# Hybrid trunk of Mamba, HGRN2 and gated DeltaNet layers: chunk states on 32-row tiles of the array, Mamba's column halves in turn and its first decays later

## The chip, the cores and the metric

One core of a Trainium2 chip runs the whole program in one launch. The metric is the device time of that core in microseconds, the median of several runs.

## The reference

A trunk of four residual layers on 256 tokens of width 1024, followed by an RMSNorm. Layers 0 and 3 mix tokens with Mamba-2, layer 1 with HGRN2, layer 2 with gated DeltaNet; after its mixer each layer has cross-attention into 256 memory tokens and a gated feed-forward block with a short convolution. The change touches Mamba and HGRN2:

```python
# Mamba-2, per group of 4 heads (8 groups, heads of width 64)
decay = exp(where(causal, acum[l] - acum[s], -inf))
cb = einsum('lk,sk->ls', cc, bc)                   # shared by the 4 heads
y = einsum('ls,sp->lp', cb * decay, x * dt)
y = rmsnorm_per_group((y + d_skip * x) * silu(z))

# HGRN2, per head (8 heads of 128), chunks of 32 tokens
gc = cumsum(log_f)                                 # inside a chunk
att = where(causal, (q * exp(gc)) @ (k * exp(-gc)).T, 0)
o = att @ v + (q * exp(gc)) @ state
state = state * exp(gc[-1])[:, None] + (k * exp(gc[-1] - gc)).T @ v
```

## The kernel before, in words

**Products.** Every large projection is three fp32r products of 128x128x256 on TensorE (lines 168 to 170; `mm3`): weights come in by DMA on SP's queue as `raw`, ScalarE casts them to `wH` (line 160), VectorE takes the rest `wL` = raw - wH (line 161). These products are the stream into which all else is set.

**Weaving.** The mixers' small work is written as generators. Class `Weave` (lines 56 to 94) keeps a clock that advances by the estimated time of each product; a generator yields (cost, latency), and its next step is issued when the clock has passed that latency. So the numbers in `ML` (Mamba) and `HL` (HGRN2) and those at the yields decide between which products a small step lies. The engines then run their own lists in that order, and semaphores hold an engine whose operand is late.

**Mamba** (one group g of the eight): `columns` (line 563) transposes the cumulated decays into `tcol`. `decays` (line 579) builds four tiles `E` of 128x384 from `rb` and `tcol` on VectorE (lines 589, 591), and ScalarE takes their exponential (line 593). `group` (line 595) then has three steps. The first transposes x (`xt`, line 600), multiplies C by B (`cb`, lines 603, 604), and masks it into `cbm`, partly on VectorE (line 607) and partly by a copy on ScalarE (line 609). GpSimd multiplies the four E by `cbm` (line 614). The second step has the output products `yp` (lines 622, 623), two heads side by side on 64 columns of the array each; VectorE, ScalarE (`msq`, line 628) and GpSimd (`s`, line 630) prepare the norm of the group. The third step is the product `gn` with ones (line 633) and the scaling.

**HGRN2** (one pair of heads, four pairs): `pair` (line 710) transposes the decayed keys (`kp`, copied to `ket` on ScalarE, line 717), multiplies q by k (`ap`, masked into `att` on VectorE, line 726), and computes the chunk states: each burst `sp` (line 735) multiplies 128 rows of `ket` by `vb`, in which GpSimd (line 812) has put v once per chunk, zero outside that chunk, so that one product of 512 or 384 columns gives four or three chunk states. VectorE chains them into `S` (lines 741, 743). The output bank `op` gets the products of `att` (line 752) in one step and those of the states (line 759) in two more; then `token_norm` and the transposes `bp` follow. Four PSUM banks (tag `mx`) hold all of these small products in turn, the other four (`acc`) the large ones.

Of the kernel before, what the change touches and what calls it, by code (L numbers as in the profile page):

```python
# [8 lines left out]
F32 = mybir.dt.float32  # L9
# [77 lines left out]
def tile_trunk(ctx: ExitStack, tc: tile.TileContext, io: dict, out: bass.AP, layers=range(DEPTH), parts="mxf", final=True):  # L87
# [449 lines left out]
    def mamba(layer, ia, gname):  # L537
        with ExitStack() as ex:
# [30 lines left out]

            cols = weave.push(late(ML[0], columns()))  # L570

# [23 lines left out]
            def group(g, bx, sz, Es):  # L595
# [17 lines left out]
                for E in Es:  # L613
                    POOL.tensor_tensor(out=E, in0=E, in1=flat(cbm), op=ALU.mult)
                yield 1100, ML[2]
                y2 = yT[:, 2 * g:2 * g + 2, :]
                for i in range(2):
                    yp = mx("yp")
                    for j in range(2):
                        d = yp[64 * j:64 * j + 64]  # L620
                        E = Es[2 * i + j]
                        PE.matmul(d[:, :T], xd[:, 0, 2 * i + j, :], E[:, :256], start=True, stop=False, skip_group_check=True)
                        PE.matmul(d[:, P:T], xd[:, 1, 2 * i + j, :], E[:, 256:], start=False, stop=True, skip_group_check=True)
                    DVE.scalar_tensor_tensor(out=y2[:, i, :], in0=bx[:, 2 + i, :], scalar=pcol("m_d", ia * 16 + 2 * g + i),
                                             in1=yp[:, :T], op0=ALU.mult, op1=ALU.add)
# [16 lines left out]
            for g in range(8):  # L642
# [4 lines left out]
                for u in range(3):  # L647
                    ps = bank("mps")
                    proj([io["m_in"][ia, 6 * g + 2 * u + i] for i in range(2)], ps)
                    with tc.high_priority(offset=EVAC):  # L650
                        if u == 2:
                            exp_ln_tables(ACT.activation(out=bx, in_=cc, func=AF.Silu),
                                          ACT.activation(out=flat(sz), in_=ps, func=AF.Silu))
                            continue
                        for i in range(2):
                            ti = [16 + g, 24 + g, 2 * g, 2 * g + 1][2 * u + i]
                            conv(cc[:, 2 * u + i, :], ps[:, i * T:(i + 1) * T], lambda j: pcol("m_cw", (ia * 32 + ti) * 4 + j),
                                 4, pcol("m_cb", ia * 32 + ti))
                    if g == 0 and u == 1:
                        weave.finish([cols])  # L660
                    if u == MU:
                        if g >= 2:
                            weave.finish([gens[g - 2]])
                        decays(g, Es)
# [4 lines left out]
    def hgrn(layer, ib, gname):  # L669
        with ExitStack() as ex:  # L670
            wk = ex.enter_context(phase(f"hw{layer}", 2))
            U = lambda shape, nm: wk.tile(shape, F32, tag=nm, name=nm, bufs=1)
            oT = U([P, KT, T], "hoT")
            hc = U([P, 388], "hc")
            nc.scalar.dma_start(out=hc, in_=io["cm"][:, CM["bd"]:CM["bd"] + 388])

# [32 lines left out]

            def pair(pr, ki, ke, eg, v, vb, qd, sg):  # L710

# [16 lines left out]

                Ss = []
                for i in range(2):  # L730
                    S = wk.tile([P, 7, P], F32, tag=f"S{i}", name=f"S{i}", bufs=1)
                    for half in range(2):
                        sp = mx("sp")
                        nch = 4 - half
                        PE.matmul(sp[:, :nch * P], ket[:, i, half * P:(half + 1) * P],
                                  vb[:, half, :nch, i * P:(i + 1) * P], start=True, stop=True)
                        for c4 in range(nch):
                            c = 4 * half + c4
                            src = sp[:, c4 * P:(c4 + 1) * P]
                            if c == 0:  # L740
                                DVE.tensor_copy(S[:, 0, :], src)
                            else:
                                DVE.scalar_tensor_tensor(out=S[:, c, :], in0=S[:, c - 1, :],
                                                         scalar=eg[:, i, 32 * c + 31:32 * c + 32], in1=src,
                                                         op0=ALU.mult, op1=ALU.add)
                    yield 1600, HL[1]
                    Ss.append(S)
                op = mx("op")
                for i in range(2):
                    for mt in range(2):  # L750
                        a = 2 * i + mt
                        PE.matmul(op[:, a * P:(a + 1) * P], att[:, a, :], v[:, mt, i * P:(i + 1) * P],
                                  start=a == 0, stop=False, skip_group_check=True)
                yield 870, HL[2]
                for i in range(2):
                    for c in range(1, 8):
# [3 lines left out]
                                  start=False, stop=True, skip_group_check=True)  # L760
                    yield 1530, HL[3] if i == 0 else 0
                on = token_norm(wk, op)
                yield 0, HL[4]

# [9 lines left out]
            for pr in range(4):  # L774
# [34 lines left out]
                ACT.copy(flat(v), ps)  # L809
                vb = wk.tile([P, 2, 4, T], F32, tag="vb", name="vb", bufs=1)  # L810
                for c4 in range(4):
                    POOL.tensor_scalar(out=vb[:, :, c4, :], in0=v, scalar1=hc[:, 384 + c4:385 + c4], scalar2=None, op0=ALU.mult)

# [11 lines left out]
                                         op0=ALU.mult, op1=ALU.mult)  # L825
                gens.append(weave.push(late(HL[5], pair(pr, ki, ke, eg, v, vb, qd, sg))))
            return out_proj(io["h_out"][ib], KT, oT, [gens[:2], gens[2:]], gname, layer)
# [514 lines left out]
```

## Time and profile before

| | us |
|---|---|
| runs | 2039.07, 2039.09, 2043.4 (median 2039.09) |
| profiled execution | 2039.35 |
| its span, first to last instruction | 2037.6 |
| TensorE busy in the span | 1987.2 (98%) |
| VectorE, ScalarE, GpSimd busy | 1575.0, 1280.4, 341.6 |

The span is covered by the matmul engine nearly everywhere, so the profile is read by the places where its stream of large products is held up. A place of that kind is a burst of small products: the time from the start of the last large product ahead of it to the start of the second one behind it, less two ordinary steps, is what the burst takes out of the stream. Columns of a timeline row are the start (us from the beginning of the span), the time of the group (us), engine, line, operation, tiles, shape, count; in brackets stands the idle time ahead and what ended it.

### The profile page before, as it was taken

The numbers are of one execution on the slowest core, as the hardware profiler recorded it, in microseconds if no ns is written. First come the engines' busy times: TensorE is split into PE (matmuls) and PEld (weight loads), VectorE is DVE, ScalarE is ACT, GpSimd is POOL, SyncE is SP. The second block draws the span as 40 slices with busy tenths as digits, with TensorE's granted clock in tenths as the row PEclk, the third lists the DMA queues.
The fourth block names the chain that finished last, engine by engine and source line by source line (L and its number), as shares of the span: only waits on it lengthen the run. The fifth ranks groups of instructions, "written<-read, shape, count | busy, mean of one in ns | idle before, by whom it ended". The sixth has DMA issues, their size and how long they took to land.

```text
span 2037.6 us, 42013 instructions
## 1 busy us (share of the span) xinstructions
PE 1987.2 (98%) x17020; PEld 1942.3 (95%) x17020; DVE 1575.0 (77%) x2417; ACT 1280.4 (63%) x1874; POOL 341.6 (17%) x468
## 2 busy tenths in 40 slices
PE   8999999999999999999999999999999999999997
PEld 8999999999999899999998899999999999999997
DVE  6899777875788778866786875878756999777875
ACT  6687666654565566555676875666545778666553
POOL 2032211000133110001064451110001133201001
PEclk9999999999999999999999999999999999999999
DMA  7655545666644546666544333457666565545663
GB/s 242 202 186 173 174 146 167 216 193 181 211 156 135 150 133 211 200 192 192 188 123 136 107 111 123 140 162 217 193 177 200 196 197 171 179 136 176 195 193 121
DMA packets 112770, 351.53 MB, mean 173 GB/s; under 512 B 15744, under 2 KB 25664, under 8 KB 112576
## 3 DMA queue, kind: packets, MB, share of 16 engines
q1 hardware_dynamic: 106176, 333.42, 52.9%
q10 hardware_dynamic: 6144, 15.17, 2.2%
q8 instruction: 133, 2.18, 0.4%
q0 software_dynamic: 256, 0.26, 0.1%
q14 instruction: 61, 0.50, 0.1%
HBM read 344.81 MB, written 4.00 MB: 171 GB/s over the span
## 4 chain that ended last, share of the span: by engine, by line
PE 78%; issue 5%; DVE 5%; ACT 4%; POOL 2%; DMA 1%; DVEq 0%; SPq 0%; POOLq 0%; ACTq 0%
PE ffps L170 8%; PE ffps L169 8%; PE ffps L168 8%; PE acc L168 6%; PE acc L169 6%; PE acc L170 6%; PE mps L168 4%; PE mps L170 3%; PE mps L169 3%; DVE wL L161 2%; PE qps L170 2%; PE qps L168 2%; PE qps L169 2%; PE kvps L168 1%; PE kvps L170 1%
## 5 line engine op out<-in xcount | busy, mean ns | idle before, releaser
L161 DVE TENSOR_TENSOR wL<-raw,wH 128x1024 fp32r<-128x1024 f32 (+2 forms) x639 | 786.3, 1232 | 326.8 <-ACT wH L160 324.3
L160 ACT CAST wH<-raw 128x1024 fp32r<-128x1024 f32 (+2 forms) x639 | 658.9, 1032 | 535.6 <-PE ffps L169 160.8
L168 PE MATMUL ffps<-hH,wH 128*128 128x256 f32 x1376 | 380.6, 277 | 0.0
L169 PE MATMUL ffps<-hL,wH 128*128 128x256 f32 x1376 | 379.8, 276 | 0.0
L170 PE MATMUL ffps<-hH,wL 128*128 128x256 f32 x1376 | 379.2, 276 | 0.0
L168 PE MATMUL acc<-aH,wH 128*128 128x256 f32 x1232 | 344.5, 280 | 0.0
L170 PE MATMUL acc<-aH,wL 128*128 128x256 f32 x1232 | 341.4, 277 | 0.6 <-DVE wL L161 0.6
L169 PE MATMUL acc<-aL,wH 128*128 128x256 f32 x1232 | 341.0, 277 | 0.0
L169 PEld LDWEIGHTS ffps<-hL,wH 128*128 128x128 f32 x1376 | 258.3, 188 | 0.1
L168 PEld LDWEIGHTS ffps<-hH,wH 128*128 128x128 f32 x1376 | 258.3, 188 | 0.1
L170 PEld LDWEIGHTS ffps<-hH,wL 128*128 128x128 f32 x1376 | 258.0, 188 | 0.0
L168 PEld LDWEIGHTS acc<-aH,wH 128*128 128x128 f32 x1232 | 231.5, 188 | 1.3 <-issue 0.7
L170 PEld LDWEIGHTS acc<-aH,wL 128*128 128x128 f32 x1232 | 231.3, 188 | 1.1 <-DVE wL L161 1.0
L169 PEld LDWEIGHTS acc<-aL,wH 128*128 128x128 f32 x1232 | 231.6, 188 | 0.6
L168 PE MATMUL mps<-hH,wH 128*128 128x256 f32 x768 | 218.0, 284 | 0.0
L169 PE MATMUL mps<-hL,wH 128*128 128x256 f32 x768 | 213.8, 278 | 0.0
L170 PE MATMUL mps<-hH,wL 128*128 128x256 f32 x768 | 213.0, 277 | 0.0
L212 POOL TENSOR_TENSOR ns<-nsq 128x256 f32<-128x256 f32 x13 | 10.7, 821 | 856.7 <-ACT nsq L209 856.7
L168 PEld LDWEIGHTS mps<-hH,wH 128*128 128x128 f32 x768 | 144.3, 188 | 2.9 <-issue 2.4
L169 PEld LDWEIGHTS mps<-hL,wH 128*128 128x128 f32 x768 | 144.4, 188 | 0.7
L170 PEld LDWEIGHTS mps<-hH,wL 128*128 128x128 f32 x768 | 144.4, 188 | 0.3
L170 PE MATMUL gps<-hH,wL 128*128 128x256 f32 x448 | 127.6, 285 | 0.6 <-DVE wL L161 0.6
(410 smaller groups left out, 4670.1 us busy)
## 6 DMA issues: line engine op xcount, KB each, us to landing
raw<-f_up SPq DMA_DIRECT2D x176, 512.0 KB, 4.1
raw<-m_in SPq DMA_DIRECT2D x96, 512.0 KB, 3.6
raw<-f_down SPq DMA_DIRECT2D x80, 512.0 KB, 4.2
raw<-xa_kv SPq DMA_DIRECT2D x60, 512.0 KB, 4.3
raw<-g_in SPq DMA_DIRECT2D x48, 512.0 KB, 4.1
raw<-m_out SPq DMA_DIRECT2D x32, 512.0 KB, 3.6
raw<-xa_q SPq DMA_DIRECT2D x32, 512.0 KB, 3.6
raw<-xa_o SPq DMA_DIRECT2D x32, 512.0 KB, 3.6
```

The lines of the kernel that those rows point to most:

```text
L160: ACT.copy(H[:, c], raw[:, c])
L161: DVE.tensor_tensor(out=L[:, c], in0=raw[:, c], in1=f32(H[:, c]), op=ALU.subtract)
L168: PE.matmul(dst, aH, bH, start=start, stop=False, skip_group_check=True)
L169: PE.matmul(dst, aH, bL, start=False, stop=False, skip_group_check=True)
L170: PE.matmul(dst, aL, bH, start=False, stop=stop, skip_group_check=True)
L212: self.eng.tensor_tensor(out=self.sum, in0=sq[:, :T], in1=sq[:, T:], op=ALU.add)
```

## The change

Two parts, in two mixers.

Mamba: `columns` gets 2000 ns more ahead of it. The output products go by column half (c) with the two heads inside, where before each head had both of its halves in a row. The first two groups yield 3000 and 700 ns more before their output products. The decays of group 0 are computed one projection step later (u = 2 in place of u = 1).

HGRN2: the masked copies `vb` and the mask columns of `hc` are gone. The chunk states are 14 products per pair, each of 32 rows (the tokens of one chunk) by 128 columns, with 128 columns moving; chunk row r of both heads and halves goes into bank `sps[r]`, so all four `mx` banks are held at once. The two copies of a pair's first state go to ScalarE. The output products are one step, 4 of `att` and 14 of the states, after one latency of 5000 ns.

```diff
@@ -567,7 +567,7 @@
                 ACT.copy(flat(tcol), tp[:, :128])
                 yield 110, 0
 
-            cols = weave.push(late(ML[0], columns()))
+            cols = weave.push(late(ML[0] + 2000, columns()))
 
             rbs = []
 
@@ -612,15 +612,16 @@
                                   in1=tcol[:, :, 32 + 4 * g:36 + 4 * g].unsqueeze(3).to_broadcast([P, 2, 4, 64]), op=ALU.mult)
                 for E in Es:
                     POOL.tensor_tensor(out=E, in0=E, in1=flat(cbm), op=ALU.mult)
-                yield 1100, ML[2]
+                yield 1100, ML[2] + (3000, 700)[g] if g < 2 else ML[2]
                 y2 = yT[:, 2 * g:2 * g + 2, :]
                 for i in range(2):
                     yp = mx("yp")
-                    for j in range(2):
-                        d = yp[64 * j:64 * j + 64]
-                        E = Es[2 * i + j]
-                        PE.matmul(d[:, :T], xd[:, 0, 2 * i + j, :], E[:, :256], start=True, stop=False, skip_group_check=True)
-                        PE.matmul(d[:, P:T], xd[:, 1, 2 * i + j, :], E[:, 256:], start=False, stop=True, skip_group_check=True)
+
+                    for c in range(2):
+                        for j in range(2):
+                            k = 2 * i + j
+                            PE.matmul(yp[64 * j:64 * j + 64, c * P:T], xd[:, c, k, :], Es[k][:, c * T:T + c * P],
+                                      start=c == 0, stop=c == 1, skip_group_check=True)
                     DVE.scalar_tensor_tensor(out=y2[:, i, :], in0=bx[:, 2 + i, :], scalar=pcol("m_d", ia * 16 + 2 * g + i),
                                              in1=yp[:, :T], op0=ALU.mult, op1=ALU.add)
                 DVE.tensor_tensor(out=y2, in0=y2, in1=sz, op=ALU.mult)
@@ -651,14 +652,13 @@
                         if u == 2:
                             exp_ln_tables(ACT.activation(out=bx, in_=cc, func=AF.Silu),
                                           ACT.activation(out=flat(sz), in_=ps, func=AF.Silu))
-                            continue
-                        for i in range(2):
+                        for i in range(2 if u < 2 else 0):
                             ti = [16 + g, 24 + g, 2 * g, 2 * g + 1][2 * u + i]
                             conv(cc[:, 2 * u + i, :], ps[:, i * T:(i + 1) * T], lambda j: pcol("m_cw", (ia * 32 + ti) * 4 + j),
                                  4, pcol("m_cb", ia * 32 + ti))
-                    if g == 0 and u == 1:
+                    if g == 0 and u == 2:
                         weave.finish([cols])
-                    if u == MU:
+                    if u == (MU if g else 2):
                         if g >= 2:
                             weave.finish([gens[g - 2]])
                         decays(g, Es)
@@ -671,8 +671,8 @@
             wk = ex.enter_context(phase(f"hw{layer}", 2))
             U = lambda shape, nm: wk.tile(shape, F32, tag=nm, name=nm, bufs=1)
             oT = U([P, KT, T], "hoT")
-            hc = U([P, 388], "hc")
-            nc.scalar.dma_start(out=hc, in_=io["cm"][:, CM["bd"]:CM["bd"] + 388])
+            hc = U([P, 384], "hc")
+            nc.scalar.dma_start(out=hc, in_=io["cm"][:, CM["bd"]:CM["bd"] + 384])
 
             A = lambda nm: U([P, 8], f"lb_{nm}")
             raw = [prm[:, PO["lb"] + 8 * i:PO["lb"] + 8 * i + 8] for i in range(DEPTH)]
@@ -707,7 +707,7 @@
             rst = hc[:, P:P + T]
             W = lambda nm, b=2: wk.tile([P, 2, T], F32, tag=nm, name=nm, bufs=b)
 
-            def pair(pr, ki, ke, eg, v, vb, qd, sg):
+            def pair(pr, ki, ke, eg, v, qd, sg):
 
                 kp = mx("kp")
                 for i in range(2):
@@ -726,41 +726,38 @@
                 DVE.copy_predicated(out=att, mask=bdm, data=ap.rearrange("p (a b) -> p a b", a=4))
                 yield 1300, HL[0]
 
-                Ss = []
-                for i in range(2):
-                    S = wk.tile([P, 7, P], F32, tag=f"S{i}", name=f"S{i}", bufs=1)
-                    for half in range(2):
-                        sp = mx("sp")
-                        nch = 4 - half
-                        PE.matmul(sp[:, :nch * P], ket[:, i, half * P:(half + 1) * P],
-                                  vb[:, half, :nch, i * P:(i + 1) * P], start=True, stop=True)
-                        for c4 in range(nch):
-                            c = 4 * half + c4
-                            src = sp[:, c4 * P:(c4 + 1) * P]
-                            if c == 0:
-                                DVE.tensor_copy(S[:, 0, :], src)
-                            else:
-                                DVE.scalar_tensor_tensor(out=S[:, c, :], in0=S[:, c - 1, :],
-                                                         scalar=eg[:, i, 32 * c + 31:32 * c + 32], in1=src,
-                                                         op0=ALU.mult, op1=ALU.add)
-                    yield 1600, HL[1]
-                    Ss.append(S)
+                sps = [mx("sp") for r in range(4)]
+                for b in range(4):
+                    i, half = divmod(b, 2)
+                    for r in range(4 - half):
+                        t = slice(32 * r, 32 * r + 32)
+                        PE.matmul(sps[r][:, b * P:(b + 1) * P], ket[t, i, half * P:(half + 1) * P],
+                                  v[t, half, i * P:(i + 1) * P], start=b == 0, stop=True, skip_group_check=True)
+                Ss = [wk.tile([P, 7, P], F32, tag=f"S{i}", name=f"S{i}", bufs=1) for i in range(2)]
+                for i, S in enumerate(Ss):
+                    for c in range(7):
+                        src = sps[c % 4][:, (2 * i + c // 4) * P:(2 * i + c // 4 + 1) * P]
+                        if c == 0:
+                            ACT.copy(S[:, 0, :], src)
+                        else:
+                            DVE.scalar_tensor_tensor(out=S[:, c, :], in0=S[:, c - 1, :],
+                                                     scalar=eg[:, i, 32 * c + 31:32 * c + 32], in1=src,
+                                                     op0=ALU.mult, op1=ALU.add)
+                yield 1000, 5000
                 op = mx("op")
                 for i in range(2):
                     for mt in range(2):
                         a = 2 * i + mt
                         PE.matmul(op[:, a * P:(a + 1) * P], att[:, a, :], v[:, mt, i * P:(i + 1) * P],
                                   start=a == 0, stop=False, skip_group_check=True)
-                yield 870, HL[2]
                 for i in range(2):
                     for c in range(1, 8):
                         a = 2 * i + c // 4
                         r = slice(32 * (c % 4), 32 * (c % 4) + 32)
                         PE.matmul(op[r, a * P:(a + 1) * P], qd[:, i, 32 * c:32 * c + 32], Ss[i][:, c - 1, :],
                                   start=False, stop=True, skip_group_check=True)
-                    yield 1530, HL[3] if i == 0 else 0
                 on = token_norm(wk, op)
-                yield 0, HL[4]
+                yield 1900, HL[4]
 
                 bp = mx("bp")
                 for i in range(2):
@@ -807,9 +804,6 @@
                 proj_tok([io["h_in"][ib, pr, 2 + kh] for kh in range(2)], ps)
                 v = W("v")
                 ACT.copy(flat(v), ps)
-                vb = wk.tile([P, 2, 4, T], F32, tag="vb", name="vb", bufs=1)
-                for c4 in range(4):
-                    POOL.tensor_scalar(out=vb[:, :, c4, :], in0=v, scalar1=hc[:, 384 + c4:385 + c4], scalar2=None, op0=ALU.mult)
 
                 ps = bank("qps")
                 proj([io["h_in"][ib, pr, 4 + i] for i in range(2)], ps)
@@ -823,7 +817,7 @@
                 exp_ln_tables(sq, ACT.activation(out=flat(sg), in_=ps, func=AF.Silu))
                 DVE.scalar_tensor_tensor(out=flat(qd), in0=flat(qd), scalar=float(128 ** -0.5), in1=flat(eg),
                                          op0=ALU.mult, op1=ALU.mult)
-                gens.append(weave.push(late(HL[5], pair(pr, ki, ke, eg, v, vb, qd, sg))))
+                gens.append(weave.push(late(HL[5], pair(pr, ki, ke, eg, v, qd, sg))))
             return out_proj(io["h_out"][ib], KT, oT, [gens[:2], gens[2:]], gname, layer)
 
     def token_norm(wk, op):
```

On ScalarE, in Mamba's group 0, the copy of `cbm` (line 609 in both) stands before the change right behind that group's last exponential (`rb`, `mrow`: the next group's decays; `sz`, `bx`, `cc`: SiLU and convolutions):

```order
L593 ACTIVATE E<-E 128x384
L609 COPY cbm<-cb 128x128
L577 DMA rb<-mrow_763 128x1024
L160 CAST wH<-raw 128x1024
L329 ACTIVATE cc<-mps,prm 128x256
L653 ACT_TABLE_LOAD
L653 ACTIVATE sz<-mps 128x512
```

and with the change:

```order
L593 ACTIVATE E<-E 128x384
L577 DMA rb<-mrow_763 128x1024
L160 CAST wH<-raw 128x1024
L329 ACTIVATE cc<-mps,prm 128x256
L654 ACT_TABLE_LOAD
L654 ACTIVATE sz<-mps 128x512
L160 CAST wH<-raw 128x1024
L653 ACTIVATE bx<-cc 128x1024
L198 ACT_TABLE_LOAD
L160 CAST wH<-raw 128x1024
L609 COPY cbm<-cb 128x128
L329 ACTIVATE cc<-mps,prm 128x256
```

It has moved behind a DMA issue, three casts of weights, a convolution step, two SiLUs (`sz`, and `bx` of the next group) and two table loads.

On TensorE the output products of group 0 stood between large products (`mps`), 55 of them ahead of the next group's `xt`. The order before:

```order
L168 MATMUL mps<-hH,wH 128x256
L169 MATMUL mps<-hL,wH 128x256
L170 MATMUL mps<-hH,wL 128x256
L622 MATMUL yp<-E,xd 64x256
L623 MATMUL yp<-E,xd 64x128
L622 MATMUL yp<-E,xd 64x256
L623 MATMUL yp<-E,xd 64x128
L622 MATMUL yp<-E,xd 64x256
```

and with the change:

```order
L169 MATMUL mps<-hL,wH 128x256
L170 MATMUL mps<-hH,wL 128x256
L623 MATMUL yp<-E,xd 64x256 x2
L623 MATMUL yp<-E,xd 64x128 x2
L623 MATMUL yp<-E,xd 64x256 x2
L623 MATMUL yp<-E,xd 64x128 x2
L600 MATMUL xt<-ident,bx 128x128 x4
L603 MATMUL cb<-bx 128x128
L604 MATMUL cb<-bx 128x256
L168 MATMUL mps<-hH,wH 128x256
```

They have moved 63 large products back, and `xt` and `cb` of group 1 follow without a large product between. `gn` of group 0 now comes 27 large products behind `cb` (39 before), and `yp` of group 1 six behind that `gn` (26 before).

On TensorE in HGRN2's first pair, before the change, the chunk states lie in two bursts, six large products apart (`fps`, `ips`: projections; `att`, `S`, `qd`: operands of the output):

```order
L170 MATMUL fps<-hH,wL 128x256
L735 MATMUL sp<-vb,ket 128x512
L735 MATMUL sp<-vb,ket 128x384
L168 MATMUL fps<-hH,wH 128x256
L169 MATMUL fps<-hL,wH 128x256
L170 MATMUL fps<-hH,wL 128x256
L168 MATMUL fps<-hH,wH 128x256
L169 MATMUL fps<-hL,wH 128x256
L170 MATMUL fps<-hH,wL 128x256
L735 MATMUL sp<-vb,ket 128x512
L735 MATMUL sp<-vb,ket 128x384
L168 MATMUL fps<-hH,wH 128x256
```

and with the change one burst of 14:

```order
L168 MATMUL fps<-hH,wH 128x256
L169 MATMUL fps<-hL,wH 128x256
L170 MATMUL fps<-hH,wL 128x256
L734 MATMUL sp<-v,ket 128x128 x14
L168 MATMUL fps<-hH,wH 128x256
L169 MATMUL fps<-hL,wH 128x256
```

Behind it come 48 large products, and then all products of `op` together:

```order
L170 MATMUL ips<-wH,hL 128x256
L751 MATMUL op<-v,att_7121 128x128 x4
L757 MATMUL op<-S_7461,qd 32x128 x7
L757 MATMUL op<-S_7462,qd 32x128 x7
L168 MATMUL ips<-wH,hH 128x256
```

## Rows read from the trace of the kernel before

**Rows 1.** The page: busy time of each engine (us, share of the span, instructions), and the engines' shares of the chain that ended last.

```profile
PE 1987.2 (98%) x17020; PEld 1942.3 (95%) x17020; DVE 1575.0 (77%) x2417; ACT 1280.4 (63%) x1874; POOL 341.6 (17%) x468
...
PE 78%; issue 5%; DVE 5%; ACT 4%; POOL 2%; DMA 1%; DVEq 0%; SPq 0%; POOLq 0%; ACTq 0%
```

**Rows 2.** Timeline of TensorE, a later burst of `yp` (layer 0, group 2) with the large products on both sides.

```profile
135.74 0.28 PE L170 MATMUL mps<-hH,wL 128*128 128x256 f32 x1
135.94 0.66 PE L622 MATMUL yp<-E,xd 128*64 128x256 f32 x4
136.43 0.40 PE L623 MATMUL yp<-E,xd 128*64 128x128 f32 x4
...
137.67 0.28 PE L169 MATMUL mps<-hL,wH 128*128 128x256 f32 x1
```

**Rows 3.** The same for `yp` of group 0 of layer 0.

```profile
95.77 0.28 PE L170 MATMUL mps<-hH,wL 128*128 128x256 f32 x1
95.98 0.65 PE L622 MATMUL yp<-E,xd 128*64 128x256 f32 x2
...
99.67 0.28 PE L169 MATMUL mps<-hL,wH 128*128 128x256 f32 x1
```

**Rows 4.** Timeline of GpSimd, groups 0 and 1 of layer 0.

```profile
94.18 4.41 POOL L614 TENSOR_TENSOR E<-E,cbm 128x384 f32<-128x384 f32 x4 [61.07 <-ACT cbm L609]
111.39 0.74 POOL L630 TENSOR_TENSOR s<-msq 128x256 f32<-128x256 f32 x1 [12.79 <-ACT msq L628]
112.07 4.90 POOL L614 TENSOR_TENSOR E<-E,cbm 128x384 f32<-128x384 f32 x4
```

**Rows 5.** Timeline of ScalarE around the `cbm` copy of group 0.

```profile
93.86 0.25 ACT L609 COPY cbm<-cb 128x128 f32<-128x128 f32 x1
95.31 1.05 ACT L160 CAST wH<-raw 128x1024 fp32r<-128x1024 f32 x1 [1.20 <-PE mps L169]
...
98.13 0.60 ACT L653 ACTIVATE sz<-mps 128x512 f32<-128x512 f32 x1
...
102.86 1.28 ACT L652 ACT_TABLE_LOAD   x1
104.16 1.06 ACT L652 ACTIVATE bx<-cc 128x1024 f32<-128x1024 f32 x1
```

**Rows 6.** Timeline of VectorE after it.

```profile
97.64 2.03 DVE L161 TENSOR_TENSOR wL<-raw,wH 128x1024 fp32r<-128x1024 f32 x1
...
100.84 0.47 DVE L331 SCALAR_TENSOR_TENSOR cc<-mps,prm,cc 128x253 f32<-128x253 f32 x1
...
103.19 1.22 DVE L161 TENSOR_TENSOR wL<-raw,wH 128x1024 fp32r<-128x1024 f32 x1
104.33 0.68 DVE L626 TENSOR_TENSOR yT<-yT,sz 128x512 f32<-128x512 f32 x1
```

**Rows 7.** Waits of the weight loads over the whole span: us in total, times, longest us.

```profile
PEld yp L622 <- POOL E L614: 1.8, 6, 0.4
...
PEld gn L633 <- POOL s L630: 1.3, 2, 0.6
```

**Rows 8.** Windows of TensorE around `yp` of group 1 and of a later group: length in us, busy time (instructions), granted clock, DMA share, GB/s.

```profile
115.70:117.72 2.02, 2.02 (x18) 1.00 0.88 247
135.85:137.42 1.57, 1.57 (x18) 1.00 0.24 86
```

**Rows 9.** Windows in the DeltaNet layer, same columns.

```profile
1069.90:1073.10 3.20, 0.00 (x0) 0.90 0.39 130
1072.50:1079.30 6.80, 6.11 (x27) 0.50 0.86 290
```

**Rows 10.** Timeline of TensorE, pair 0 of HGRN2: for each of four bursts the last large product ahead, the burst, the second large product behind.

```profile
578.19 0.28 PE L170 MATMUL fps<-hH,wL 128*128 128x256 f32 x1
578.96 1.74 PE L735 MATMUL sp<-vb,ket 128*128 128x512 f32 x4 [0.49 <-ACT ket L717]
...
580.66 0.28 PE L169 MATMUL fps<-hL,wH 128*128 128x256 f32 x1
...
581.12 0.28 PE L170 MATMUL fps<-hH,wL 128*128 128x256 f32 x1
581.24 1.67 PE L735 MATMUL sp<-vb,ket 128*128 128x512 f32 x4
...
582.86 0.28 PE L169 MATMUL fps<-hL,wH 128*128 128x256 f32 x1
...
583.34 0.28 PE L170 MATMUL fps<-hH,wL 128*128 128x256 f32 x1
583.46 1.05 PE L752 MATMUL op<-v,att 128*128 128x128 f32 x8
...
584.47 0.28 PE L169 MATMUL fps<-hL,wH 128*128 128x256 f32 x1
...
586.97 0.28 PE L170 MATMUL ips<-wH,hL 128*128 128x256 f32 x1
587.18 0.64 PE L759 MATMUL op<-S,qd 128*32 128x128 f32 x14
...
587.97 0.28 PE L169 MATMUL ips<-wL,hH 128*128 128x256 f32 x1
```

**Rows 11.** Instructions that touch the tile `sp`: the chain of states on VectorE, ns min/median/max, first and last start, shape.

```profile
L743 DVE SCALAR_TENSOR_TENSOR S<-S,eg,sp x48: 336/348/350, 581.4 to 673.4; 128x128 f32<-128x128 f32 x48
```

## Prediction

> **What bounds the kernel.** I read the page first: TensorE is busy for 98% of the span and makes up 78% of the chain of work that ended last; GpSimd is busy for 17% [rows 1]. So only what TensorE is given to do, or what it waits for, can move the time; VectorE, ScalarE and GpSimd count where TensorE stands waiting for them. Next the timelines of TensorE around the touched bursts. The measure of a burst is the start of the second large product behind it less that of the last one ahead, less two steps of the stream of 0.115 us (four of them lie between 580.66 and 581.12 [rows 10]). Third, the lists of the other engines at the same places, for what ends the waits.
>
> A steady burst of `yp` costs 137.67 - 135.74 - 0.23 = 1.70 us [rows 2]; that of group 0 costs 3.67 [rows 3], so 1.97 of it is waiting. Group 1's window is 2.02 long where a steady one is 1.57 [rows 8]: 0.45 of waiting. The four products `E` of group 0 end on GpSimd at 94.18 + 4.41 = 98.59 [rows 4], 2.71 after TensorE came free at 95.88: the wait is that lateness less some 0.74, the work that can be done between. Group 1 agrees: 112.07 + 4.90 = 116.97 is 1.27 after 115.70, which less 0.74 is 0.53, against 0.45 seen. The weight loads show it as GpSimd's `E` being waited for, and `gn` waiting for `s`, 1.3 us in two layers [rows 7].
>
> In HGRN2's pair 0 the bursts cost 2.24 us (`sp`, 0.73 of it for `ket`, since the next one costs 1.51), 1.51 (`sp`), 0.90 (`att`) and twice 0.77 (states; one of the two is shown) [rows 10].
>
> **HGRN2, part by part.** *Chunk states.* A pair now streams 512 and 384 columns for each of two heads, in two passes: 1792 columns in 1.51 us, so 128 columns pass in 0.108 us, and a pair costs 2 x 1.51 = 3.02. The new 14 products are 28 passes of 128 columns on four row tiles; the busiest tile has 4 products, 8 passes, 0.86 us, if the four run side by side. What a burst on small tiles costs beside its passes comes from the products of the states on four 32-column tiles: 7 products put two on the busiest tile, 4 passes or 0.43 us, and the burst costs 0.77 [rows 10], so 0.34. Sum 0.86 + 0.34 = 1.20, a gain of 1.82 a pair. No row of this trace shows 32-row tiles of 128 columns; one after another they would cost 28 x 0.108 + 0.34 = 3.36, a loss of 0.34. I take the side-by-side end, because the column tiles, the nearest row, do run so: 14 passes in a row would take 1.5 us, and they took 0.64. The Trainium skill ("TensorE: Matmul & The Clock Gate", Part 3, the table of measured speedups) gives 3.07 times for four row tiles at 512 columns; by that, an estimate, the burst would be 3.02 / 3.07 + 0.34 = 1.32 and the gain 1.70.
>
> *Output in one step.* Before 0.90 + 0.77 + 0.77 = 2.44; now the same passes with one change of tile shape in place of two, 0.90 + 2 x 0.43 + 0.34 = 2.10: a gain of 0.34 a pair. In pair 1 the last product of the states stands apart, 36 products later: 0.5 lost. Nothing or the whole 0.34 are the ends.
>
> *What is late next.* The wait of 0.73 for `ket` stays: `sp` is still six products behind `kp`. The chain of states is 12 steps of 0.35 us [rows 11] with one or two weight remainders of 1.22 [rows 6] between, 5.4 to 6.6 us and a copy ahead of it. Its cover is 48 products, 5.5 us, and the 0.9 of `att`; 0 to 0.5 a pair remains, I take 0.2. The four `mx` banks are all held meanwhile; the next small step on a bank is `op` itself, behind the same cover.
>
> *`vb` gone, copies on ScalarE, the shorter `hc`.* Nothing: GpSimd stands at 17%, `vb` was never what TensorE waited for at `sp`, and eight copies of some 0.3 us lie beside ScalarE's idle time. The cover is the large products; without it, the copies would stand ahead of weight casts.
>
> Sum: 4 x (-1.82 - 0.34 + 0.2) + 0.5 = -7.3 us, between -9 and -4 while the tiles run side by side.
>
> **Mamba, part by part.** *Column order.* In the steady burst all four passes over 256 columns start ahead of all four over 128 [rows 2], although each head's 256 and 128 stand in a row in the program before: the two heads already run side by side. The floor is 3072 columns / 2 / 1.19 = 1.29 us, and 1.70 less 0.34 is 1.36. So nothing, with 0.07 a burst as the end.
>
> *`columns` later, decays later.* The transposes stay behind the same large product in the order on TensorE, so nothing there. The later decays move VectorE's and ScalarE's rows of group 0 by little.
>
> *The later `yp`.* It is meant to give GpSimd time: 63 products or 7.2 us, so TensorE arrives at 95.88 + 7.2 = 103.1. But `cbm`, which GpSimd's chain waits for, was copied at 93.86 and now stands on ScalarE behind the SiLUs, two table loads and the casts. From `sz` on: 98.13 + 0.60 + 1.05 (cast) + 1.06 (`bx`) + 1.28 (table) + 1.05 (cast) + 0.25 (copy) = 103.4 [rows 5]. That is the early end; `bx` needs the last convolution step, 100.84 + 0.47 now [rows 6], of which 0.8 is due to a remainder that took 2.03 beside GpSimd in place of 1.22; 100.5 gives 104.1. GpSimd's four products then end at 103.4 + 4.41 = 107.8, 4.7 after TensorE came, and the wait is 4.7 - 0.74 = 3.95 in place of 1.97: **+2.0**. A remainder going first on VectorE would add up to 1.2.
>
> *Group 0's norm and group 1's `yp`.* The burst ends near 108.5. VectorE's two steps (each as a convolution step, 0.47) and product with `sz` (0.68) [rows 6], ScalarE's square (as `sz`, 0.60 [rows 5]) and GpSimd's `s` (0.74 [rows 4]) give 111.5, or 112.4 with other work between; TensorE reaches `gn` at 108.5 + 1.1 + 27 x 0.115 = 112.7, the 1.1 being `xt` and `cb`, whose 896 columns take 0.75 us in one pass and 1.5 in two. So most of the 0.65 a layer that `gn` waits goes: -0.5. GpSimd starts group 1's products behind `s`, near 112.2, and ends 4.4 to 4.9 later, near 116.9; TensorE comes only six products behind `gn`, near 113.9. Lateness 3.0, wait 2.3 in place of 0.45: **+1.9**, between +1.0 and +3.0. `xt` right behind `yp` saves one change of tile shape, -0.34.
>
> Per layer 2.0 + 1.9 - 0.5 - 0.34 = +3.1, between +1.6 and +5.5; layer 3 has the same order, so +6.2 for both.
>
> **Sum.** The profiled execution took 2039.35 us, 0.26 over the median of 2039.09. 2039.35 - 7.3 + 6.2 = 2038.25; I say **2038.2**, no change that can be measured: a run of this kernel tells 0.2%, or 4.1 us, from nothing, which puts "faster" below 2035.0 and "slower" above 2043.2. The two sums' ends, not both at once, give 2033.5 to 2044.
>
> **Rivals.**
> *The row tiles don't overlap (0.1), slower.* The price is 3.36 in place of 1.20 at `sp`, 2.16 x 4 = 8.6 us: 2046.8. It decides from 2.5 us a burst on. For it: no row shows such tiles. Against: the column tiles.
> *The Mamba waits go as meant (0.15), faster.* If `cbm` comes early enough on ScalarE, by its casts running ahead by 4 us, the waits of 1.97, 0.45 and 0.65 and a change of shape (0.34) go in both layers: 3.4 x 2 = 6.8 in place of +6.2, so 2025.2. Against: its place behind the SiLU of `bx`, whose convolution ends no earlier than 100.
> *The clock falls (0.1), slower.* After TensorE's 3.2 us of idleness ahead of 1073.1 the granted clock is 0.50, the lower level of 1.2 GHz, for 6.8 us, which costs 3.4 [rows 9]. The waits of 3.95 are of that length, though single passes lie between; in one layer 2041.6, in both 2045.
> *The column order matters (0.05), faster.* If the passes ran strictly as written, two heads could overlap only at the seams, and the new order would free up to 0.28 us (1.57 [rows 8] less the floor) in 16 bursts: 4.5, so 2033.8. The Trainium skill says just that of matmuls ("TensorE: Matmul & The Clock Gate", Part 3, what overlaps and what doesn't: strict order, no reordering). The rows of the steady burst disagree: the second head's passes start before the first head's shorter ones.
>
> **How the numbers follow.** My forecast has 0.6, and of that a sixth or so lies beyond the bounds on either side: 0.05 below 2035.0, 0.08 above 2043.2. Faster: 0.15 + 0.05 + 0.05 = 0.25. Slower: 0.1, half of 0.1, and 0.08 = 0.23. The rest, 0.52, is no change. The range leaves out the case of the vanished waits and the far side of the serial tiles: 2032 to 2045.
>
> **What would show it.** In the changed profile: `sp` bursts of 1.2 us (3.4: the tiles are serial); bursts of `op` of 2.1; GpSimd's first `E` of group 0 at 103 to 105 and released by the `cbm` copy (by 99: the waits have gone); `yp` of group 0 costing 5.3 with `xt` to be taken off, that of group 1 near 4.0; steady `yp` still 1.70; no window at 0.50 near 105. I am wrong if the Mamba stage of a layer changes by less than 1 us or a pair of HGRN2 gains less than 1.

## The result, and the profile after

| | us |
|---|---|
| forecast | 2038.2, range 2032 to 2045 |
| kernel before, 4 runs | 2041.24 median (2039.07 to 2049.8) |
| changed kernel, 4 runs | 2068.82 median (2063.6 to 2076.7) |
| ratio | 1.013, interval 1.0084 to 1.0177 |
| the profiled execution after | 2076.7, span 2074.8 |

28 us slower, outside the range. (Two single runs of over 4000 us, one of the kernel before and one of an experiment, and the slowest run of `e2_mamba`, 2087.07 us, are left out of all figures below.) The bursts answer first, since the forecast rests on them. HGRN2's pair 0 on TensorE, timeline of the changed kernel, columns as ahead:

```profile
591.38 0.28 PE L170 MATMUL fps<-hH,wL 128*128 128x256 f32 x1
591.58 1.23 PE L734 MATMUL sp<-v,ket 32*128 32x128 f32 x28
592.75 0.38 PE L168 MATMUL fps<-hH,wH 128*128 128x256 f32 x1
592.97 0.28 PE L169 MATMUL fps<-hL,wH 128*128 128x256 f32 x1
...
598.39 0.28 PE L170 MATMUL ips<-wH,hL 128*128 128x256 f32 x1
598.51 1.05 PE L751 MATMUL op<-v,att 128*128 128x128 f32 x8
599.49 1.07 PE L757 MATMUL op<-S,qd 128*32 128x128 f32 x28
600.49 0.39 PE L168 MATMUL ips<-wH,hH 128*128 128x256 f32 x1
600.72 0.28 PE L169 MATMUL ips<-wL,hH 128*128 128x256 f32 x1
```

`sp` costs 592.97 - 591.38 - 0.23 = 1.36 us where the two bursts of [rows 10] cost 3.75, and `op` 2.10 where three cost 2.44. Over the four pairs, by the same subtraction, `sp` goes from 12.9 to 6.6 us and `op` from 9.8 to 8.9: -7.1. In pair 3 the burst is split by a wait:

```profile
674.78 0.71 PE L734 MATMUL sp<-v,ket 32*128 32x128 f32 x10
676.09 0.94 PE L734 MATMUL sp<-v,ket 32*128 32x128 f32 x18 [0.59 <-DVE att L726]
```

The burst needs all four `mx` banks, one of which `ap` holds until VectorE has made `att` from it: 1.0 us in pair 3, 0.2 in pair 2. (Before, this wait stood in pair 3 alone, with 0.15.)

Mamba, layer 0, TensorE's timeline, small products alone (it answers to [rows 3] and the first row of [rows 8]):

```profile
104.63 0.65 PE L623 MATMUL yp<-E,xd 128*64 128x256 f32 x2 [1.68 <-POOL E L614]
105.59 1.60 PE L623 MATMUL yp<-E,xd 128*64 128x256 f32 x8 [0.31 <-POOL E L614]
107.50 0.86 PE L623 MATMUL yp<-E,xd 128*64 128x256 f32 x6 [0.31 <-POOL E L614]
108.29 0.66 PE L600 MATMUL xt<-ident,bx 128*128 128x128 f32 x4
...
112.84 0.70 PE L634 MATMUL gn<-s,ones 128*128 128x256 f32 x2 [0.16 <-POOL s L631]
...
114.17 1.51 PE L623 MATMUL yp<-E,xd 128*64 128x256 f32 x8
...
116.76 0.65 PE L623 MATMUL yp<-E,xd 128*64 128x256 f32 x2 [1.07 <-POOL E L614]
117.94 0.86 PE L623 MATMUL yp<-E,xd 128*64 128x256 f32 x6 [0.53 <-POOL E L614]
```

Group 0 waits for `E` longer than before, and group 1 as well. GpSimd, and ScalarE's chain ahead of the `cbm` copy (they answer to [rows 4] and [rows 5]):

```profile
102.71 4.74 POOL L614 TENSOR_TENSOR E<-E,cbm 128x384 f32<-128x384 f32 x4 [70.67 <-ACT cbm L609]
111.99 0.79 POOL L631 TENSOR_TENSOR s<-msq 128x256 f32<-128x256 f32 x1 [4.55 <-ACT msq L629]
112.74 5.14 POOL L614 TENSOR_TENSOR E<-E,cbm 128x384 f32<-128x384 f32 x4
```

```profile
97.61 0.60 ACT L654 ACTIVATE sz<-mps 128x512 f32<-128x512 f32 x1
98.11 1.04 ACT L160 CAST wH<-raw 128x1024 fp32r<-128x1024 f32 x1
99.04 1.06 ACT L653 ACTIVATE bx<-cc 128x1024 f32<-128x1024 f32 x1
100.12 1.28 ACT L198 ACT_TABLE_LOAD   x1
101.42 1.05 ACT L160 CAST wH<-raw 128x1024 fp32r<-128x1024 f32 x1
...
102.37 0.26 ACT L609 COPY cbm<-cb 128x128 f32<-128x128 f32 x1
```

Over both layers `yp`, `xt` with `cb` and `gn` cost 58.3 us before and 66.9 after: +8.6. So the bursts sum to +1.5 us, and the profiles differ by 37. The rest is in stretches that the change does not touch. Windows of 100 us in the four feed-forward stages (columns as in [rows 8]), before and after:

```profile
345.00:445.00 100.00, 100.00 (x885) 1.00 0.67 204
775.00:875.00 100.00, 100.00 (x884) 1.00 0.67 206
1370.00:1470.00 100.00, 100.00 (x885) 1.00 0.68 204
1865.00:1965.00 100.00, 100.00 (x884) 1.00 0.64 193
```

```profile
350.00:450.00 100.00, 100.00 (x851) 1.00 0.62 197
780.00:880.00 100.00, 100.00 (x852) 1.00 0.63 196
1385.00:1485.00 100.00, 100.00 (x852) 1.00 0.62 197
1895.00:1995.00 100.00, 100.00 (x851) 1.00 0.60 189
```

The engine is busy throughout and the granted clock is 1.00 in both, yet 885 products lie in 100 us before and 851 after; by their start times one starts every 113.3 ns or every 117.8. Long stretches of lines 168 to 170 without a burst or a wait in them show only these two paces. A stage and what follows it up to the next burst are some 1580 products (1487 in the last layer), 7.0 us between the paces. Over all large products (some 14,900) the mean step is 114.1 ns before and 116.4 after: 34 us of the 37.

### The profile page after: what moved, and what is told of

Same layout as the page of the kernel before. It is cut to its first block, busy times and chain, and to the rows that moved or that the text cites. A ratio compares the mean times of both kernels' runs of the same rounds, so it can differ in the third digit from the quotient of the medians.

```text
span 2074.8 us, 42149 instructions
## 1 busy us (share of the span) xinstructions
PE 2015.9 (97%) x17100; PEld 1972.7 (95%) x17100; DVE 1566.4 (75%) x2409; ACT 1275.5 (61%) x1878; POOL 308.1 (15%) x452
## 5 line engine op out<-in xcount | busy, mean ns | idle before, releaser
L168 PE MATMUL ffps<-hH,wH 128*128 128x256 f32 x1376 | 387.4, 282 | 0.0
L169 PE MATMUL ffps<-hL,wH 128*128 128x256 f32 x1376 | 386.6, 281 | 0.0
L170 PE MATMUL ffps<-hH,wL 128*128 128x256 f32 x1376 | 386.0, 281 | 0.0
L170 PEld LDWEIGHTS ffps<-hH,wL 128*128 128x128 f32 x1376 | 263.6, 192 | 0.0
```

Of the source, the lines that this page charges most:

```text
L168: PE.matmul(dst, aH, bH, start=start, stop=False, skip_group_check=True)
L169: PE.matmul(dst, aH, bL, start=False, stop=False, skip_group_check=True)
L170: PE.matmul(dst, aL, bH, start=False, stop=stop, skip_group_check=True)
```

## The experiments

In the diffs "-" and "+" are against the kernel named. A range is over the runs of that kernel.

**Is the pace the program's?** The changed kernel again, unaltered, with 12 runs, beside 35 of the kernel before on the same chip.

> The changed kernel itself, once more. In its first profile 14900 large products start 116.4 ns apart on the mean, 114.1 in the kernel before; that alone is 34 of the 37 us between the two profiled runs. Theory A (the pace of a stage is a property of the program): the same stages show 117.8 again, all four feed-forward stages among them, and the time is 2063 to 2077. Theory B (it falls anew in each execution): some of the feed-forward stages show 113.3, each worth 7 us, and the runs spread from 2042 to 2077.

2054.72 (2046.77 to 2071.04) against 2052.05 (2038.23 to 2065.05): ratio 1.0023, interval 0.9994 to 1.0052. Theory B. Its feed-forward stages:

```profile
350.00:450.00 100.00, 100.00 (x885) 1.00 0.67 203
775.00:875.00 100.00, 100.00 (x885) 1.00 0.66 205
1370.00:1470.00 100.00, 100.00 (x884) 1.00 0.67 205
1875.00:1975.00 100.00, 100.00 (x851) 1.00 0.61 190
```

The same program, three stages quick and one slow. The kernel before, too, spreads over 27 us. So the pace of these stages falls anew in each execution. That most of the first measurement's 28 us came of it is shown for the two executions that were profiled, no slow stage against four; for the others it is argued from this spread. What the change does had to be sought apart from it.

**The parts alone.** Three kernels take the change apart: the hunks of its diff from `hc` on (e1_hgrn), those ahead of it (e2_mamba), and of these the loop over c and j alone (e3_order).

> The HGRN2 part alone. By the sum of the prediction -7 us, 2032. If one part brings the slow pace and it is this one: up to 2065, with the feed-forward stages of layers 1 to 3 at 117.8 and that of layer 0, which lies ahead of HGRN2, at 113.3. If the pace belongs to the Mamba part: 2032.

> The Mamba part alone. By the sum of the prediction +6, 2045; with the 10 us that the two Mamba stages cost in the changed kernel's profile 2049. If the slow pace comes with the Mamba part: 2070 to 2080, all four feed-forward stages at 117.8. If it falls anew in each execution, anything between.

> The column order of yp alone, no later decays. Prediction: nothing, 2039. In the changed kernel the 34 large products behind each steady yp start 117.8 apart, 113.6 in the kernel before: if the order of the burst sets the pace behind it, these stretches are slow here too, 0.15 us each, and less than 5 us in all; if it brings the slow pace of the feed-forward stages as well, 2065.

In this order 2046.08 (ratio 0.9969, 0.9935 to 1.0003), 2066.25 (1.007, 1.0029 to 1.011) and 2051.37 (0.9998, 0.9969 to 1.0027). With 7 us a stage by chance the times tell little; the profiles tell more. HGRN2's bursts give the same -7.1. The column order takes `yp` from 1.70 to 1.65 in a steady group. But with it the large products behind `xt` with `cb`, and those behind `gn` up to the next `yp`, start 117.8 apart, where in the kernel before they settle at 113.3. Behind a steady `gn` of layer 0, the 6th and the 42nd large product, in the kernel before and in e3_order:

```profile
170.91 0.28 PE L170 MATMUL mps<-hH,wL 128*128 128x256 f32 x1
174.99 0.28 PE L170 MATMUL mps<-hH,wL 128*128 128x256 f32 x1
```

```profile
171.21 0.28 PE L170 MATMUL mps<-hH,wL 128*128 128x256 f32 x1
175.45 0.28 PE L170 MATMUL mps<-hH,wL 128*128 128x256 f32 x1
```

36 steps take 4.08 us in the one and 4.24 in the other. Right behind the steady `yp` itself the pace settles at 113.3 in either order, so the slow stretch that the expectation put there begins one burst later. This is no chance of an execution: it shows behind the steady bursts, from group 2's `yp` on, in both layers of all seven profiles with the new order (the changed kernel twice, and experiments here and below) and in none of the six with the old. From a layer's first `xt` to its last `gn`, what the steps have above 113.3 sums to 2.0 to 3.0 us in the seven and to 0.4 to 1.1 in the six. In the profile of the Mamba part a further thing shows, which [rows 9] priced: the clock falls behind the longer waits, here in layer 0 and layer 3, to a mean of 0.62 and 0.57 of 2.4 GHz in these windows, that is to the lower level of 1.2 GHz for most of them:

```profile
120.00:124.50 4.50, 4.50 (x26) 0.62 0.06 21
...
1663.00:1667.00 4.00, 4.00 (x22) 0.57 0.01 5
```

**The late copy.** The changed kernel, with `cbm` ahead:

```diff
+                with tc.high_priority(offset=EVAC):
-                DVE.tensor_tensor(out=cbm[:, 0::2, :], ...
+                    DVE.tensor_tensor(out=cbm[:, 0::2, :], ...
-                ACT.copy(cbm[:, 1, :], cb3[:, 1, :])
+                    ACT.copy(cbm[:, 1, :], cb3[:, 1, :])
```

> The changed kernel with the two halves of cbm ahead of the weight casts (a priority at lines 607 and 609), so that on ScalarE the copy of group 0 stands behind that group's first exponential. If the late copy is what TensorE waits for at the first output products: yp with xt of group 0 falls from 6.7-7.0 us to 2.5, group 1's yp from 4.75 to 2.5 or less, and the clock of the runs returns from 0.9957 on the mean to 0.997: -7 to -14 us against the changed kernel, so 2043 to 2050. If the wait stems from GpSimd's own work, or from group 0's decays that come a step later: 6 us or more stay at group 0. The stretch from xt to gn stays at 117.8 in both cases, since the column order stays.

2060.73 against 2044.66 of the kernel before (ratio 1.0082, 1.0059 to 1.0105). The first half of the expectation held in the main: `yp` and `xt` of group 0 fell from 6.7 to 2.75 + 1.10, `yp` of group 1 from 4.75 to 3.2 (2.5 or less was expected). The time did not fall. GpSimd's queue and TensorE's waits:

```profile
108.31 3.97 POOL L615 TENSOR_TENSOR E<-E,cbm 128x384 f32<-128x384 f32 x4 [9.26 <-ACT cbm L610]
112.24 1.70 POOL L632 TENSOR_TENSOR s<-msq 128x256 f32<-128x256 f32 x1
```

```profile
PE gn L635 <- POOL s L632: 10.8, 4, 3.0
```

```profile
114.00:119.00 5.00, 5.00 (x29) 0.66 0.42 112
```

With the priority, group 1's four `E` went ahead of group 0's `s` on GpSimd, so `gn` now waits up to 3.0 us in one piece, its bursts cost 3.2 to 4.1 in place of 0.8 to 0.9, and the clock falls behind it (0.66 in the window; 0.992 to 0.995 over the runs, 0.997 for the kernel before). The copy was what `yp` waited for; taking that wait away made a worse one.

**What sets the pace.** In every slow or quick feed-forward stage the pace is there a few products after the stream resumes from the wait of 0.9 to 1.3 us at the stage's head, and it stays to the stage's end. Not every burst changes it: the two products of `ps_nrm` some 85 products later leave it as it was in all 28 stages of the seven profiles so far, ten of them slow. Two kernels test whether another burst does, with one of their own, in the kernel before:

```diff
-                proj([io["f_up"][layer, 2 * t + i] for i in range(2)], ps, t == 0)
+                mm = proj([io["f_up"][layer, 2 * t + i] for i in range(2)], ps, t == 0)
+                if t == 0:
+                    rp = mx("rp")
+                    m2 = PE.matmul(rp[:, :P], ident, ones, start=True, stop=True, skip_group_check=True)
+                    behind([m2], [mm])
```

Here `behind` orders without a semaphore; `proj` hands back its last product. That is p2_full; p1_halves has in the same place:

```diff
-                    m2 = PE.matmul(rp[:, :P], ident, ones, start=True, stop=True, skip_group_check=True)
-                    behind([m2], [mm])
+                    for j in range(2):
+                        m2 = PE.matmul(rp[64 * j:64 * j + 64, :P], ident[:, :64], ones, start=True, stop=True,
+                                       skip_group_check=True)
+                        behind([m2], [mm])
+                        mm = m2
```

> The kernel before, with two small products (64 columns of the array each, 128 moving, into a bank that nobody reads) behind the 32nd product that follows each feed-forward stage's last wait. Theory A (the pace is drawn where the stream resumes, kept until the next interruption, and a burst on column halves mostly resumes at 113.3, as 30 of 32 bursts of yp did in the kernels with the old order): at least 7 of 8 feed-forward stages in the profiles at 113.3, 0.4 us more a stage, runs 2036 to 2050 with a mean some 10 us below the kernel before. Theory B (the pace comes from elsewhere: the chip, the transfers, the place of the code): no stage changes its pace at the new burst, and the mean is 2053.

> The same with one small product on the whole array (128 x 128, 128 moving) in that place. Theory A in its narrow form (the shape of the burst decides the pace behind it): as full-array bursts (gn, xt with cb) resume at 117.8 first, all or most of the stages are slow, mean 2060 or more. In its wide form (any interruption draws anew): half of the stages slow, mean 2052. Theory B: 2052, no change of pace at the burst.

p1_halves: 2042.47 (2040.88 to 2050.77); p2_full: 2040.92 (2039.24 to 2041.77), the kernel before on that chip 2044.66 (2038.26 to 2048.65). In both profiles all four stages are quick behind the burst, and in p2_full two were slow ahead of it. The first of them, with 18 steps ahead of the burst and 30 behind it:

```profile
331.25 0.28 PE L170 MATMUL ffps<-hH,wL 128*128 128x256 f32 x1
...
333.37 0.28 PE L170 MATMUL ffps<-hH,wL 128*128 128x256 f32 x1
333.49 0.38 PE L505 MATMUL rp<-ones,ident 128*128 128x128 f32 x2
333.63 0.37 PE L170 MATMUL ffps<-hH,wL 128*128 128x256 f32 x1
333.84 0.28 PE L168 MATMUL ffps<-hH,wH 128*128 128x256 f32 x1
...
334.07 0.28 PE L170 MATMUL ffps<-hH,wL 128*128 128x256 f32 x1
...
337.47 0.28 PE L170 MATMUL ffps<-hH,wL 128*128 128x256 f32 x1
```

By the same subtraction as above the burst takes 0.24 us out of the stream, and the step goes from 117.8 to 113.3. The narrow form of theory A fell: the stream behind the full-array product was quick 4 times of 4, not slow, and the runs spread over 2.5 us where those of the kernel before spread over 10. Three of p1_halves' twelve runs lie 7 us above its others, so its burst seems not to work each time; no profile shows one of these three.

**The change's own effect.** With that product in each kernel the chance of the stages is gone. Each is a kernel of above with the lines of p2_full's diff: the changed one, e1_hgrn, e3_order, and e2_mamba with the loop of `yp` as before (r_late). All four on one chip:

> The changed kernel with the small full-array product of p2_full in each feed-forward stage, so that these stages run at 113.3 in every execution; beside p2_full (the kernel before with the same, 2040.6 on the mean of its runs) it gives the change's own effect without 7 us by chance per stage. From the rows of the profiles: bursts of Mamba +8.7, bursts of HGRN2 -7.1, the slow stretch from xt to gn behind the new column order +3.3, clock 0 to +5: 2045.5 to 2050.5. By the prediction's sum (-1.1): 2039.5. If the change also made the feed-forward stages slow by more than chance: as the first.

> The HGRN2 part alone, with the small product in each feed-forward stage. By the bursts of e1_hgrn (sp 6.6 and op 8.9 in place of 12.9 and 9.8) -7.1 against p2_full: 2033.5, and the fastest of all kernels so far; by the prediction's sum -7.3, the same. If the gain is given back elsewhere in the layer: 2037 or more.

> The column order alone, with the small product. If the stretch from xt to gn starts at 117.8 because of the order of the burst ahead: 2040.6 + 3.3 - 0.4 = 2043.5. If that pace was chance: 2040.2. The prediction (nothing): 2040.6.

> The later first output products and decays alone, in the old column order, with the small product. Bursts +9 (group 0's yp with xt +2, group 1's yp +2.6, gn +0.1 a layer, less 0.3 for 12 steady bursts that stay at 1.70), clock 0 to +5 us, stretches from xt to gn at 113.3 as before: 2049.5 to 2055. By the prediction's sum (+6.2): 2047.

| with the small product | median | range | mean |
|---|---|---|---|
| p2_full (kernel before) | 2040.92 | 2039.24 to 2041.77 | 2040.6 |
| r_hgrn | 2032.79 | 2030.88 to 2035.95 | 2033.1 |
| r_order | 2043.69 | 2042.30 to 2046.66 | 2043.8 |
| r_late | 2051.34 | 2049.13 to 2051.74 | 2051.0 |
| r_after | 2047.58 | 2045.24 to 2050.24 | 2047.5 |

In the profiles of these four all sixteen stages are quick behind the small product; two were slow ahead of it. p2_full ran on another chip than the rest; the lowest runs of the kernel before were 2038.3 there and 2037.5 here, so each difference from it may be off by some 0.8 us. The parts are -7.5, +3.2 and +10.4, together +6.1; the whole is +6.9 of 2040.6, 0.3% slower. Against the kernel before itself, with its slow stages in it, r_after is at 1.0025 (1.0012 to 1.0038) and r_hgrn at 0.9954 (0.9937 to 0.9972): HGRN2's part with the small product beats both kernels, by some 0.4%.

## Why the prediction was wrong

**The missed term.** The sum put nothing on the large products: "less two steps of the stream of 0.115 us", one step for the whole program. There are two steps, 113.3 and 117.8, and 14,900 of them; a stage is 7.0 us apart. The profile before held it, in stretches that the rows do not show: its feed-forward stages are all quick, but other stretches are slow, such as these 123 steps in 14.48 us:

```profile
41.46 0.28 PE L170 MATMUL kvps<-wH,mL 128*128 128x256 f32 x1
...
55.94 0.28 PE L170 MATMUL kvps<-wH,mL 128*128 128x256 f32 x1
```

And the three runs shown, two of them 0.02 us apart, hid that a run can be 27 us off. The bound of 0.2% for what a measurement can tell was too small for four runs: with 35 the kernel before spans 1.3%. A range from its bursts alone could not hold 2068.82; for the change itself, +6.9 on 2039.35 makes 2046.3, 1 us beyond its end. Both sums' high ends at once would have given that (2039.35 - 4 + 11 = 2046.4); the 2044 of the prediction left it out, while its 2033.5 does take both low ends. In the second measurement, at a ratio of 1.0023, "no change" would have come true, but by luck: the stages' pace hid +6.9.

**HGRN2: right.** -7.3 was forecast, -7.1 in the bursts, -7.5 in the runs. `sp` at 1.36 lay by the 1.20 worked out from column tiles, far from the serial 3.36. The estimate by the Trainium skill's table ("TensorE: Matmul & The Clock Gate", Part 3, measured speedup) was 1.32, which the trace bears out with 1.36. `op` came at 2.10 as forecast, pair 1's lone product cost 0.53. The 0.73 for `ket` did not stay in pair 0, and the chain of states (0.2 a pair) made no wait; in their place stood one for `att`'s bank, 1.2 us in two pairs, from the four banks that the prediction saw held and looked for only at `op`.

**Mamba's waits: right in place and cause, short in size (the second step that failed).** The copy was to land at 103.4 to 104.1 and came at 102.6; GpSimd ended at 107.45 (107.8); group 0's `yp` with `xt` rose by 1.9 (forecast +2.0 less 0.34). Group 1's `yp` rose by 2.6 (+1.9, bound 3.0). Of the 1.2 us a layer that the sum fell short, 0.7 lie at this `yp` and the rest mostly at `gn`: group 0's fell by 0.3, not 0.5, and group 1's, which the sum left out, rose from 0.44 to 0.87, waiting for an `s` that stands late on GpSimd, too. +4.3 a layer in place of +3.1.

**"Nothing, with 0.07 a burst as the end" for the column order: right for the burst, wrong for what follows it.** The burst gained 0.05. From the next burst, `xt` with `cb`, to the next `yp` the stream runs at the slow pace, in the steady groups of every profile with the new order: +3.2 us in the runs. The rival of strict order was worth 0.28 a burst: it did not come. That rival was put beside a rule of the Trainium skill ("TensorE: Matmul & The Clock Gate", Part 3, what overlaps and what doesn't), which the trace of these column tiles does not bear out: in [rows 2] four passes of line 622, two heads' worth, start from 135.94 on, and the first of line 623 at 136.43.

**The clock rival came in part.** Its place was right (the lower level behind the Mamba waits, 4 us long), in some executions: the changed kernel's runs have 0.9957 on the mean, the kernel before 0.9971, which on 2050 us is 2.9 us. With the small product r_after has 0.9958, r_late 0.9969 and p2_full 0.9974: the +10.4 of r_late is nearly all bursts (+9.7 in its profile), and some 3 of r_after's us are clock.

**What stays open.** What in the first products decides between 113.3 and 117.8 was not found: at the head of the feed-forward stages other engines' starts agree to some 10 ns between a quick and a slow stage. Nor is it known why the column order of `yp` sets the pace two bursts on, why the small product brings the quick pace where `ps_nrm` keeps the slow one, or why the same kernel is slower on one chip than on another (the kernel before: medians of 2052.05 and 2044.66 us on two chips, and only one profile of it).

## What to carry to other kernels

Divide a long stretch of equal products by their count, in several executions, before a difference between two kernels is put down to a change: a few ns a step, which fall anew in each execution at some resumptions and are fixed by the order of small products at others, can outweigh all that the change moves. Where an effect is smaller than such a spread, hold the state still in both kernels (here with one small product a stage) and compare then. When a wait for a late operand is taken away, look at what the same queue does next; a priority that brings one forward puts another behind.

## What was not expected of the hardware

The same product of 128x128x256 has two steady steps, 113.3 and 117.8 ns, at a granted clock of 1.00 and with the engine busy throughout; a small full-array product between them, 0.24 us out of the stream, left the quicker one behind it in all 20 stages profiled with it, four of which were slow ahead of it. 28 passes of 32x128 weights with 128 columns went by in a burst of 1.36 us, a pass of 128 columns taking 0.108 alone.
